# A Conformer-like layer on eight cores: four fill banks, adds on GpSimd, an early load of x, conv weights made on the chip, and conv results taken over DRAM

## The chip, the cores and the metric

The kernel runs on all 8 cores of one Trainium2 chip (dies: cores 0 to 3 and 4 to 7). Each core computes half of one of four sequences, 2048 frames plus what it needs of the past. The metric is the device time of the slowest core, in microseconds (us). Some executions of a program on all 8 cores are disturbed: a pair of cores or a whole die gets a lower TensorE clock and takes longer. I therefore quote two things: the ratio of fast runs, and the median span of the *undisturbed cores*, by which I mean, in runs of state fast, the cores whose granted clock is within 0.012 of the highest of that run. (A run's state is slow when one die is over 1% longer than the other at a lower clock, or when the run is over 1.5% above the fastest of its kernel. So a fast run can still hold a disturbed pair.)

## The reference, cut

```python
def reference(x, ...):                                   # x: (4, 4096, 1024) float32
    x = x + 0.5 * swiglu(rmsnorm(x, ffn1_norm), ffn1_gate, ffn1_up, ffn1_down)   # hidden 2816
    z = rmsnorm(x, mix_norm) @ w_in                      # q, k, v (512 each) and [a | b] for the conv
    attn_out = chunk_band_attention(q, k, v, rel_bias)   # 8 heads of 64, 576-key band, softmax
    conv_out = conformer_conv(u, ...)                    # GLU -> causal conv, width 31 -> LayerNorm -> silu
    x = x + concatenate([attn_out, conv_out]) @ w_out
    x = x + 0.5 * swiglu(rmsnorm(x, ffn2_norm), ffn2_gate, ffn2_up, ffn2_down)
    return rmsnorm(x, final_norm)
```

## The kernel before

The program holds a small scheduler. Each part of the layer (a norm, the GLU, an attention, ...) is a Python generator that yields a function "when could I go on?"; the scheduler estimates engine times with a simple model and lets the ready generator of the highest priority emit its next instructions. The result is a fixed order on each engine, with semaphores where data is handed over. If the model is wrong about a landing, an engine stands behind the wrong instruction. A core takes its frames in two groups (group 0 and group 1), each of them through the first FFN (FFN1), GLU, conv, attention, output projection and second FFN (FFN2). Weights pass through a ring in SBUF, loaded by a queue that GpSimd issues.

The norm: ScalarE squares, VectorE adds, TensorE sums over partitions, ScalarE makes the root, VectorE normalises eight tiles in one go.

```python
        def square(st, g, kc, s):
            ...
            act(sqt, xsl(g, kc, s), AF.Square, n, (xk,), (("sq", i),))
            if k < 7:
                dve(lambda h: h.tensor_tensor(out=ss, in0=ss, in1=sqt, op=ALU.add), n, ...)
        def norm_fin(st, g, s, idx):
            yield lambda: P.est("pe", (("ssb", r),), (("ps", 6 + nxt("st", 2, False)),))
            b = 6 + nxt("st", 2)                          # two fill banks: 6 and 7
            mm(b, 0, onesS, ssb_t[:, r, 0:n], n, True, True, ...)
            ...
            yield lambda: P.est("dve", (("rstd", rr),)) - 0.3
            for kc in range(8):                           # eight in one go
                dve(... scalar_tensor_tensor(hT or y <- x * gain * rstd) ...)
```

The LayerNorm of the conv's result, with its Silus and the way back to channel order:

```python
        def conv_ln(g):
            ...
            yield lambda: P.est("act", (("acc", 7),)) - 0.2
            for grp in range(16):                         # one burst, before the attention
                act(co[:, grp, 0:U], acc[:, grp, 0:U], AF.Silu, ...)
            for pc in range(2):                           # 32 small transfers in SBUF, as 32 before the conv
                for p4 in range(4):
                    for j in range(4):
                        P.dma("sp", ... c2 <- co ...)
            for s in g.main:
                for c in range(4):
                    dve(... tensor_copy: cvt <- c2 ...)   # to frame order, for the output projection
```

And the attention, in units: scores of two heads (64-row matmuls in pairs), exp on ScalarE, values on TensorE; at the end of a pair of heads the row sums go through Ln and Exp on ScalarE to a reciprocal, and VectorE multiplies. It could start only when the LayerNorm had read its two accumulator banks (flag ln45).

Names in the lines of the profile: `psA` are the four PSUM banks of gate, up and attention scores, `ps` the four others, among them the *fill banks* that all other matmuls share; `hT` is the normalised x, `xres` the x that is carried along, `sq`, `ssum` and `ssb` are squares and their sums, `rstd` is the reciprocal root made of them, `ring` holds weights, and `dreg` is a scratch region that GLU, conv and attention use in turn. PEld is the weight load of TensorE.

The softmax here doesn't subtract the row's maximum and nothing guards it: scores larger than these inputs give would overflow.

## Time and profile before

| before | |
|---|---|
| median of all 16 runs in the end | 1619.0 us (1614.9 to 1803.7) |
| a fast run | 1615 to 1621 us |
| profiled run | fast, cores 1594.8 to 1612.8 us |
| TensorE busy, idle | 1446.6 us (90%), 166 us |
| ScalarE table loads | 37 of 1283 ns |

The profile is read from the top down: the busy line names the bound (TensorE), the slices say where it has holes, the windows by stage give each hole a size, and the waits and the chain give each a cause. The lines are in the prediction below.

### The profile page before, as it was taken

How to read it: one execution, taken by the hardware profiler on the slowest of the kernel's cores; microseconds unless marked ns; L12 is line 12 of the kernel's file. 1: busy time of each engine (PE TensorE's matmuls, PEld its weight loads, DVE VectorE, ACT ScalarE, POOL GpSimd, SP SyncE). 2: the span in 40 equal slices, each digit the busy share in tenths (PEclk: the TensorE clock that was granted, in tenths of full speed). 3: DMA queues.
4: the chain of work that ended last, by engine and by line, in shares of the span. 5: the costliest groups of instructions: out<-in, count | busy, mean ns of one | idle time of the engine just before them, and what ended most of it. 6: DMA issues, size and time to landing. Idle time of an engine off the chain costs nothing.

```text
span 1612.8 us, 22367 instructions; the slowest of 8 cores (1594.8 to 1612.8 us)
## 1 busy us (share of the span) xinstructions
PE 1446.6 (90%) x8206; PEld 772.9 (48%) x8206; DVE 597.0 (37%) x1005; ACT 464.8 (29%) x791; POOL 52.1 (3%) x102
## 2 busy tenths in 40 slices
PE   4599999987688999986899999999888899999995
PEld 1255555444444466642455555445334455555542
DVE  3522222464323522256322222674533542222145
ACT  2311011231446410144310011333556631101122
POOL 0000000000000000000000000000000000000000
PEclk9799999999798999998899999999999999999997
DMA  8334215147630266518144232055610033343303
GB/s 176 93 73 85 53 27 92 27 105 124 122 69 1 53 111 111 99 37 231 23 76 86 53 65 54 11 114 105 128 37 1 1 65 60 55 78 58 66 1 130
DMA packets 26905, 119.21 MB, mean 74 GB/s; under 512 B 8112, under 2 KB 12208, under 8 KB 16816
## 3 DMA queue, kind: packets, MB, share of 16 engines
q0 software_dynamic: 14112, 93.33, 32.7%
q1 hardware_dynamic: 12688, 24.47, 4.6%
q8 instruction: 68, 1.11, 0.3%
q14 instruction: 37, 0.30, 0.1%
HBM read 198.49 MB, written 8.39 MB: 128 GB/s over the span
## 4 chain that ended last, share of the span: by engine, by line
PE 73%; DVE 9%; ACT 7%; issue 5%; DMA 5%; SPq 2%; DVEq 0%; ACTq 0%; POOL 0%; POOLq 0%
PE psA L352 45%; PE ps L352 28%; ACT dreg L356 3%; DVE hT L506 2%; DMA xres<-xin 2%; DMA ring<-wgu 2%; SPq L728 1%; ACT L356 1%; DVE ssum L466 1%; ACT sq L356 1%; DVE xres L647 1%; DVE dreg L506 1%; DMA dreg<-dreg 1%; ACT rstd L356 1%; DVE dreg L997 1%
## 5 line engine op out<-in xcount | busy, mean ns | idle before, releaser
L352 PE MATMUL psA<-hT,ring 128*128 128x384 bf16 (+2 forms) x4192 | 770.7, 345 | 25.8 <-DVE hT L506 20.3
L352 PEld LDWEIGHTS psA<-hT,ring 128*128 128x128 bf16 x4192 | 413.0, 99 | 378.5 <-issue 59.8
L356 ACT ACTIVATE dreg<-psA 128x384 f32<-128x384 f32 (+4 forms) x346 | 216.8, 631 | 773.0 <-PE psA L352 761.1
L352 PE MATMUL ps<-at,ring 128*128 128x384 bf16 (+1 forms) x1936 | 357.5, 346 | 20.1 <-DVE xres L647 20.1
L617 DVE TENSOR_TENSOR at<-psA,dreg 128x384 bf16<-128x384 f32 (+1 forms) x242 | 143.6, 594 | 517.2 <-PE psA L352 502.6
L352 PEld LDWEIGHTS ps<-at,ring 128*128 128x128 bf16 x1936 | 191.2, 99 | 184.0 <-issue 36.5
L647 DVE SCALAR_TENSOR_TENSOR xres<-ps,xres 128x384 f32<-128x384 f32 (+1 forms) x176 | 104.8, 596 | 153.6 <-PE ps L352 153.6
L356 ACT ACTIVATE sq<-xres 128x384 bf16<-128x384 f32 (+1 forms) x154 | 84.5, 552 | 180.2 <-DVE xres L647 134.8
L466 DVE TENSOR_TENSOR ssum<-ssum,sq 128x384 f32<-128x384 f32 (+1 forms) x132 | 78.5, 595 | 92.4 <-ACT sq L356 87.2
L352 PE MATMUL ps<-dreg,ring 128*128 128x384 bf16 (+3 forms) x608 | 98.3, 313 | 1.1 <-DVE xres L1054 0.6
L506 DVE SCALAR_TENSOR_TENSOR hT<-xres,cs_sb,rstd 128x384 bf16<-128x384 f32 (+1 forms) x136 | 78.8, 653 | 11.9 <-ACT rstd L356 11.9
L352 PE MATMUL ps<-hT,ring 128*128 128x384 bf16 (+1 forms) x352 | 69.8, 356 | 12.0 <-ACT at L356 6.0
L352 PEld LDWEIGHTS ps<-dreg,ring 128*128 128x128 bf16 x608 | 58.1, 101 | 30.7 <-issue 3.5
L356 ACT ACT_TABLE_LOAD x37 | 47.5, 1283 | 45.8 <-PE psA L352 25.5
L352 PE MATMUL ps<-dreg,at 128*128 128x384 bf16 (+3 forms) x216 | 45.4, 307 | 16.4 <-DVE dreg L997 10.3
L352 PEld LDWEIGHTS ps<-hT,ring 128*128 128x128 bf16 x352 | 35.1, 101 | 42.6 <-issue 18.7
L352 PE MATMUL ps<-ssb,cb_sb 128*128 128x384 bf16 (+1 forms) x22 | 8.3, 379 | 49.2 <-DVE ssb L471 49.2
L420 POOL DMA_DIRECT2D ring<-wgu x44 | 23.4, 533 | 822.5 <-PE ps L352 503.5
L356 ACT ACTIVATE dreg<-dreg 128x192 bf16<-128x192 f32 (+5 forms) x88 | 35.4, 440 | 48.7 <-DVE dreg L844 44.8
L720 DVE TENSOR_TENSOR dreg<-psA,dreg 128x384 bf16<-128x384 f32 (+2 forms) x20 | 39.5, 1995 | 16.4 <-PE psA L352 8.7
L997 DVE TENSOR_TENSOR dreg<-ps,dreg 64x384 bf16<-64x384 f32 (+1 forms) x40 | 23.3, 581 | 59.1 <-ACT dreg L356 56.5
L352 PE MATMUL ps<-ring,hT 128*128 128x512 bf16 x160 | 37.5, 391 | 4.1 <-DVE vh L665 3.0
(56 smaller groups left out, 446.4 us busy)
## 6 DMA issues: line engine op xcount, KB each, us to landing
ring<-wgu POOLq DMA_DIRECT2D x44, 1024.0 KB, 9.7
ring<-wdA POOLq DMA_DIRECT2D x16, 768.0 KB, 7.7
ring<-wdB POOLq DMA_DIRECT2D x16, 640.0 KB, 7.0
ring<-win POOLq DMA_DIRECT2D x10, 1024.0 KB, 9.2
ring<-wcv POOLq DMA_DIRECT2D x8, 1152.0 KB, 11.2
xres<-xin SPq DMA_DIRECT2D x4, 1536.0 KB, 18.6
yout<-dreg SPq DMA_DIRECT2D x3, 1536.0 KB, 6.3
ring<-wout POOLq DMA_DIRECT2D x4, 1024.0 KB, 16.7
```

The costliest lines, as they stand in the source:

```text
L352: P.op("pe", lambda h: h.matmul(o, lhsT=lhsT, rhs=rhs, start=start, stop=stop, skip_group_check=True), max(n / 2370.0, 0.06) if dur is Non ...
L356: P.op("act", lambda h: h.activation(out=out, in_=in_, func=func, **kw), 0.19 + n / 1400.0, reads, writes)
L420: P.dma("pool", lambda h, dst=dst, src=p.src: h.dma_start(out=dst, in_=src), "w%d" % (p.id % 8), 512 * p.n, reads=(), writes=(("w", p.id), ...
L466: dve(lambda h: h.tensor_tensor(out=ss, in0=ss, in1=sqt, op=ALU.add), n, (("ssum", r), ("sq", i)), (("ssum", r),))
L506: dve(lambda h, dst=dst, xin=xin, gcol=gcol: h.scalar_tensor_tensor(out=dst, in0=xin, scalar=gcol, in1=rt, op0=ALU.mult, op1=ALU.mult), n, ...
L617: dve(lambda h, at=at, ub=ub, tt=tt: h.tensor_tensor(out=at, in0=ub, in1=tt, op=ALU.mult), n, (("ps", bU), ("tmpF", ti)), (("AT", gi, fl, ...
L647: dve(lambda h, xo=xo, bk=bk: h.scalar_tensor_tensor(out=xo, in0=bk, scalar=0.5, in1=xo, op0=ALU.mult, op1=ALU.add), n, (("ps", b), xk), ( ...
L720: dve(lambda h, gd=gd, a4=a4, t4=t4: h.tensor_tensor(out=gd, in0=a4, in1=t4, op=ALU.mult), n, (("ps", bA), ("rs", ti)), (("g", c),))
L728: P.dma("sp", lambda h, src=src, dst=dst: h.dma_start(out=dst, in_=src), "gp%d" % pc, 64 * 2 * W, reads=(("g", 2 * pc), ("g", 2 * pc + 1)) ...
L997: dve(lambda h, o_=o_, i0=i0, i1=i1: h.tensor_tensor(out=o_, in0=i0, in1=i1, op=ALU.mult), n, (("ps", 4 + e), ("rs", ri)), (("q", gi, j, s),))
```

## The change

Its intent is to fill TensorE's holes. Its parts: (1) four fill banks instead of two, and normalising in steps of two tiles; (2) the adds of the sums of squares move from VectorE to GpSimd (Pool), save in the first norms; (3) the x of group 1 is loaded early into free scratch and normalised from there; (4) the 64 small transfers per group between GLU, conv and output become 24 larger ones over DRAM; (5) the conv's weights are no longer loaded but multiplied out of 576 columns, half on Pool, half on VectorE; (6) the conv's sums go to Pool instead of through 64 statistics matmuls; (7) the order is freer: the attention no longer waits for ln45, the first block's V and Q rank right behind the conv, and the Silus are given out in pairs; (8) dummy matmuls keep the clock up where the model foresees a gap. Besides, x and some of the weights arrive in smaller pieces. Cut to its core:

```diff
+        mode = {"fill": (4, 5, 6, 7), "lru": [4, 5, 6, 7]}          # (1); 6, 7 during attention
-            b = 6 + nxt("st", 2)
+            b = fb_take()
...                                                                  # norm_fin
-            yield lambda: P.est("dve", (("rstd", rr),)) - 0.3
             for kc in range(8):
+                if kc % 2 == 0:
+                    yield lambda: max(P.est("dve", (("rstd", rr),)) - 0.3, P.t["dve"] - 1.0)
...                                                                  # square (2)
+            add = dve if norm0 and g.gi == 0 else pool
...                                                                  # (3)
+        def prefetch_x(g):
+            yield lambda: 0.0 if ("wout", g.gi - 1) in F else INF
+            for s in g.ids[1:]:
+                P.dma("sp", ... xps <- xin ...)
+                S.add(0, norm_load(g, s))
...                                                                  # conv_ln (4), (7)
-            yield lambda: P.est("act", (("acc", 7),)) - 0.2
             for grp in range(16):
+                if grp % 2 == 0:
+                    yield lambda: max(P.est("act", (("acc", grp + 1),)) - 0.2, P.t["act"] - 1.0)
                 act(co[:, grp, 0:U], acc[:, grp, 0:U], AF.Silu, ...)
-            ... 32 transfers c2 <- co
+            ... 8 transfers to DRAM, 4 back (likewise for GLU to conv)
...                                                                  # attention (7)
-                    if ("Q", gi, s) not in F or ("v", gi, s) not in F or ("ln45", gi) not in F:
+                    if ("Q", gi, s) not in F or ("v", gi, s) not in F:
...                                                                  # issue_weights (5)
+                    (pool, dve)[p.src % 2](... ring <- cmp * identity, 2304 wide ...)
...                                                                  # mm (8)
+            keep_warm(gap, b)
```

## The prediction

> **What bounds the kernel now.** I read the table of cores first, to know the state: this execution is a fast one (both dies within 0.4%), so its 1612.8 us is what a fast run takes (the two fast runs: 1614.94 and 1615.3). Then the busy line, the slices, the costliest groups, the windows by stage, the waits of TensorE, and the chain and timeline around the big holes.
>
> ```profile
> PE 1446.6 (90%) x8206; PEld 772.9 (48%) x8206; DVE 597.0 (37%) x1005; ACT 464.8 (29%) x791; POOL 52.1 (3%) x102
> PE   4599999987688999986899999999888899999995
> PEclk9799999999798999998899999999999999999997
> ```
> PE is the bound, but the holes sit in a few places: the start, slices 8 to 13, 17 to 20, 26 to 31 and the end, and the clock dips in the same slices.
>
> ```profile
> 0.00:70.00 70.00, 30.65 (x106) 11.42 (x106) 28.29 (x55) 23.25 (x39) 2.46 (x8) 0.85 0.69 155
> 296.00:348.00 52.00, 44.71 (x239) 23.47 (x238) 32.50 (x56) 16.78 (x28) 1.05 (x2) 0.97 0.39 92
> 348.00:437.00 89.00, 64.74 (x413) 39.70 (x412) 40.33 (x55) 27.02 (x63) 4.22 (x8) 0.90 0.60 102
> 437.00:560.00 123.00, 108.03 (x687) 55.01 (x684) 47.22 (x87) 67.82 (x105) 2.11 (x4) 0.90 0.25 49
> 697.00:800.00 103.00, 80.73 (x381) 38.89 (x382) 55.00 (x100) 41.74 (x68) 2.11 (x4) 0.85 0.38 98
> 1003.00:1060.00 57.00, 52.41 (x270) 26.21 (x269) 36.23 (x59) 20.11 (x31) 1.59 (x3) 0.97 0.27 52
> 1060.00:1155.00 95.00, 88.34 (x501) 47.64 (x498) 56.41 (x62) 38.05 (x75) 4.22 (x8) 1.00 0.61 109
> 1155.00:1300.00 145.00, 120.87 (x819) 58.93 (x820) 57.70 (x99) 88.22 (x123) 1.06 (x2) 0.93 0.11 24
> 1547.00:1613.00 66.00, 45.75 (x225) 23.26 (x223) 39.14 (x68) 17.13 (x30) 0.00 (x0) 0.84 0.20 80
> ```
> Columns: stretch, its length, busy PE, weight load, DVE, ACT, POOL, then granted clock, DMA share, GB/s. The stages are, in order: start; end of the first FFN; GLU and conv of group 0; its attention; the change from group 0 to group 1; then for group 1 the end of FFN1, GLU and conv, attention; and the tail. Length less busy gives the idle time: 39.4, 7.3, 24.3, 15.0, 22.3, 4.6, 6.7, 24.1, 20.3 us, together 164 of the 166 us in the whole run. The FFN stretches between them are full, at clock 1.00.
>
> ```profile
> PE ps L352 <- DVE ssb L471: 49.2, 11, 18.0
> PE ps L352 <- ACT dreg L356: 28.7, 26, 12.5
> PE psA L352 <- DVE hT L506: 20.3, 32, 4.4
> PE ps L352 <- DVE xres L647: 20.1, 12, 5.3
> PE ps L352 <- DVE dreg L997: 15.7, 20, 2.3
> ```
> Columns: who waited for whom, total us, times, longest. The first line is PE waiting for the sum of squares of a norm; in truth it waits for x, as the chain says at the change of groups (20.24 us of loading x, then squares):
>
> ```profile
> 733.50 20.24 DMA xres<-xin
> ```
> The longest wait on ACT is the conv of group 0, for which the 32 small transfers from GLU order to phase order take from 367.6 to over 400 us:
>
> ```profile
> 408.68 0.57 PE L352 MATMUL ps<-dreg,cb_sb 128*128 128x192 bf16 x2 [12.47 <-ACT dreg L356]
> ```
> And the fourth line is a blocked bank: DVE writes eight normalised tiles in one go, in order, and PE stands until the accumulator is added to x:
>
> ```profile
> 1570.17 5.38 DVE L506 SCALAR_TENSOR_TENSOR dreg<-xres,cs_sb,rstd 128x512 f32<-128x512 f32 x8
> 1576.17 9.04 PE L352 MATMUL ps<-at,ring 128*128 128x384 bf16 x40 [5.26 <-DVE xres L647]
> ```
>
> **What the Trainium skill says.** (1) "TensorE: Matmul & The Clock Gate", Part 1: a warm matmul starts every N/2.4 + 2.5 ns, and after an idle window of about 3.4 us the clock halves until some 3.4 us of work have passed. The trace agrees: in one dense down-projection the chain holds 288 matmuls in 51.92 us, 180.3 ns each, and the formula for the mean width of 426.7 gives 180.3. After the first hole the weight loads of 512-wide matmuls start 0.43 us apart, then 0.21. (2) "GPSIMD Engine Reference", 3.1: an elementwise add of two fp32 inputs takes 4497 ns for 2048 elements there against 2293 on VectorE. No run here shows it (Pool does no adds yet); my estimate from it is 0.85 to 1.0 us at 384 wide, against 595 ns measured on DVE. (3) "SBUF — State Buffer", "Who interferes with whom": a DVE instruction with two SBUF inputs and a Pool instruction that reads SBUF exclude each other. The 8-tile normalisation is such a DVE instruction; silu products and residual adds read PSUM and are not. (4) "DMA: Bandwidth & Descriptors", anatomy of a DMA: about 2 us fixed per transfer. The trace's shortest GLU transfer lands in 1.9 us.
>
> **The floor.** Over all forms, count times (N/2.4 + 2.5 ns) sums to 1370 us; the 64-row score matmuls (35 us of it) run in pairs, so about 1355. 1613 - 1355 = 258 us are lost: 166 idle, the rest slow clock and small matmuls. Slow clock I estimate per stage as busy x (1 - clock): 4.6, 1.3, 6.5, 10.8, 12.1, 1.6, 0, 8.5, 7.3, sum 53 us. So 217 us lie within the change's reach.
>
> **The change part by part.** Each line: idle + slow clock now, what I leave after.
> - Start (39.4 + 4.6, leave 37 + 3): x arrives in quarters, blocks 1 and 2 in halves, and the Ln of a norm no longer queues behind the squares of the next block. But some 15 MB of x, weights and tables must still come in before blocks 1 and 2 can run, and the ring still holds four FFN pieces. Gain 4.
> - End of FFN1, both groups (11.9 + 2.9, leave 5 + 0): normalisation now in steps of two tiles (2 x 0.65 us) instead of eight, and four accumulator banks instead of two, so the 5.3 us block goes. Gain 10.
> - GLU and conv (31.0 + 6.5, leave 11 + 2): 64 small transfers per group (32 in, 32 back) become 24 larger ones over DRAM: per group 8 writes and 4 reads for GLU, 8 and 4 for conv. About 0.6 us issue each, two latencies, perhaps 10 us in all, under K's matmuls (24 x 3 remaining at some 0.19 us, 14 us). The conv weights (8 x 1152 KB at 11.2 us) are no longer loaded but multiplied out, half on Pool (2304 elements, estimate 5 us), half on DVE (2304/0.96, 2.4 us), 4 each per group, ahead of use. The 64 statistics matmuls (formula 7.0 us) and 32 ACT copies go; 15 pairs of Pool adds per group replace them. Gain 24 + 7.
> - Attention (39.1 + 19.3, leave 24 + 8): it no longer waits for the conv's LayerNorm banks, and conv, V and Q fill it. Its own chain of scores, exp (1.03 us each), values and reciprocal (waits of 2.0 to 2.3 us on L997) stays. Gain 26.
> - Change of groups (22.3 + 12.1, leave 4 + 2): x of blocks 1 and 2 of group 1 is loaded into the free scratch during FFN2 and normalised before the old x is gone. The 20.24 us load leaves the path. Gain 28.
> - Tail (20.3 + 7.3, leave 11 + 2): the bank stalls of 5.26 and 3.66 us go; from the last product to the output (1602 to 1613) it stays. Gain 15.
> - 154 sum-of-squares adds (91.6 us) leave DVE except 24 in the first norms; off the path, save the last of each norm: + 0.4 us x about 12 = 5.
> - Dummy matmuls fill gaps that the scheduler's own model foresees, to hold the clock. Where the model is wrong they delay real work: + 4.
>
> Sum: 4 + 10 + 31 + 26 + 28 + 15 = 114, less 9: 105 to 108. 1613 - 108 = 1505.
>
> **The rivals.** *Pool becomes the hidden bound.* It would carry some 130 adds x 1 us, 60 conv adds x 0.6, 8 x 5 us of weights: about 220 us, 14% of the span, but bunched: at the change of groups 40 adds x 1 us against 26 us of down-projection, in order with the weight transfers it issues. For: in-order queue, shared port. Against: three FFN pieces of block 0 (20 us) can run meanwhile. It would give back 20 to 30 us: 1525 to 1535. *The dummies and the scheduler's model miss.* The order on PE is fixed beforehand; if real landings differ, PE stands behind the wrong item or 90 dummies. For: at the start the model counts on a constant written earlier than the trace's 4.9 us. Against: there PE waits for data anyway. 1530 to 1560. *All holes close.* Fillers suffice and the clock stays full: floor 1348 + start 40 + tail 11 + small-matmul loss 30 + 30 = 1460. *Nothing moves:* the DRAM detour and ACT's exp replace each wait by another; against it, the 20 us load and the 5.3 us blocks go by data dependence, not by luck.
>
> **Range and chances.** 1505 us for a fast run; 1463 (near the best case) to 1558 (second rival) should hold it 8 times in 10. For "within 2%" three quarters of the gain must be lost, though the parts are independent: 4%. Slower by over 2%: 2%. Faster by over 2%: 94%. In the slow state, which two of the four runs before had, all is longer; I predict the fast one.
>
> **What would show it.** Right: no x load in the chain at the change of groups; waits on xres under 1 us; no 12 us hole before conv; PE waits on the sum of squares only at the start; Pool near 15% busy; busy PE higher than 90% of the span, with a new group of 256-wide matmuls (dummies); clock over 0.97 in the attention stages. Wrong: Pool adds over 1.3 us, or PE waits on Pool of several us per norm; gu weights landing late because their issue queues behind adds; attention stages as long as before (123 and 145 us with the same matmuls); the start longer than 70 us.

## The result and the profile after

| | before | after |
|---|---|---|
| median, all runs | 1619.0 us (16 runs) | 1558.6 us (11 runs, 1533.5 to 1773.5) |
| runs with no disturbed core | 1614.9 to 1621 | 1533.47, 1533.58, 1536.68, 1536.69 |
| undisturbed cores, median | 1609 | 1530 |
| ratio of the fast runs | | 0.9515 [0.9475, 0.9556] |

The result was correct and the change is faster. Ratios in this document are the mean time of one kernel's fast runs over that of the other's fast runs of the same rounds, so not quite the ratio of the quoted medians. The run that was profiled is disturbed on cores 6 and 7 only (1551.9 and 1557.1 us at clock 0.967 and 0.965; the others 1527.5 to 1534.0), so from here I compare core 0 with core 0: 1603.3 us before, 1529.4 after.

The page of the kernel after, its busy line and the slices of the clock:

```profile
PE 1470.7 (94%) x8558; PEld 810.6 (52%) x8558; DVE 554.9 (36%) x886; ACT 458.2 (29%) x758; POOL 276.8 (18%) x313
...
PEclk9999999999999999998888999999989999999998
```

TensorE fills 94% of a shorter span (91% without the dummies), and Pool went from 3% to 18%. The dips of the clock around the conv and the attention of group 0 are gone. Those in slices 19 to 22 lie on the disturbed core whose page this is, core 0 has none there; the one in slice 30, in the attention of group 1, core 0 has too. Groups of instructions that the change made or touched, after and (last two lines) before; columns: line, engine, operation, tiles, shapes, count, busy us, mean ns of one, idle before and its cause:

```profile
L569 POOL TENSOR_TENSOR ssum<-ssum,sq 128x384 f32<-128x384 f32 (+1 forms) x114 | 121.0, 1061 | 192.1 <-ACT sq L418 183.9
L606 DVE SCALAR_TENSOR_TENSOR hT<-xres,cs_sb,rstd 128x384 bf16<-128x384 f32 (+1 forms) x120 | 87.5, 781 | 9.4 <-ACT rstd L418 9.4
L405 PE MATMUL ps<-cb_sb 128*128 128x256 bf16 x412 | 50.4, 282 | 4.9 <-DVE cb_sb L1237 4.9
```

```profile
L506 DVE SCALAR_TENSOR_TENSOR hT<-xres,cs_sb,rstd 128x384 bf16<-128x384 f32 (+1 forms) x136 | 78.8, 653 | 11.9 <-ACT rstd L356 11.9
```

A Pool add takes 1.06 us (predicted 0.85 to 1.0 at a width of 384; at that width it is 1.01 on core 0, the mean has wider ones in it). The normalising product on VectorE went from 653 to 781 ns. These means mix widths; for the same form on core 0 it is 612 to 678 ns at 384 and 746 to 975 at 512. That Pool's reading is the cause is shown by the run addsdve below: with the adds off Pool the two are 611 and 744 again. L405 are the dummies, 50 us of TensorE that is no work. The waits of TensorE on core 0 after (who waited for whom, us, times, longest):

```profile
PE ps L414 <- ACT dreg L418: 19.0, 15, 6.4
PE ps L414 <- POOL ssb L574: 17.8, 9, 2.7
PE ps L414 <- DVE dreg L1133: 11.7, 19, 4.3
PE ps L414 <- DVE dreg L970: 8.7, 3, 5.9
```

The wait for x behind VectorE's sums (47.9 us on this core before) and the one for a blocked bank (DVE xres, 19.6 us before) have left the top of the list. But for the first this holds in part only: 27.2 of the 47.9 us were in the first 70 us, where x arrives, and there the dummies now cover the wait. Without them (run nowarm below) 29.3 us stand in the same place. What leads now is ScalarE in the attention, then Pool.

**Where the time went, stage by stage.** Because V and the end of the conv now run inside the attention, the lengths of stages can't be compared. So I take the loss of each stage: its length less the ideal time of the real matmuls in it, which is the count of each shape times (N/2.4 + 2.5 ns), half for the 64-row pairs, and nothing for dummies. Stage borders are from core 0's timeline, to about 1 us; FFN1 ends with its last down-projection. The prediction took its numbers from core 7, the slowest one, so its column is compared to about that. The spans fell by 79 us in the median of the undisturbed cores, by 74 on core 0, which was a short one before.

| stage | loss before | after | gain | predicted |
|---|---|---|---|---|
| start, up to the first down-projection | 42.2 | 43.4 | -1 | 4 |
| FFN1 from its first down-projection, both groups | 17.6 | 5.8 | 12 | 10 |
| norm, GLU, K and conv, both groups | 46.1 | 24.4 | 22, and 7 of matmuls that went | 31 |
| attention and output projection, both groups | 80.5 | 75.3 | 5 | 26 |
| FFN2 of group 0 and start of FFN1 of group 1 | 34.4 | 16.5 | 18 | 28 |
| FFN2 of group 1 and output | 26.2 | 14.3 | 12 | 15 |
| sum | 247.0 | 179.7 | 74 | 114 less 9 |

74 us is the difference of the two spans. The attention is the large miss. Windows of core 0 over the attentions of groups 0 and 1, first before, then after (length; busy us of PE, weight load, DVE, ACT, Pool; clock; DMA share; GB/s):

```profile
445.00:518.00 73.00, 58.16 (x427) 29.17 (x427) 22.96 (x44) 45.06 (x63) 0.53 (x1) 0.90 0.13 27
1155.00:1275.00 120.00, 103.33 (x722) 50.14 (x720) 47.76 (x82) 77.57 (x105) 0.53 (x1) 0.91 0.07 14
```

```profile
412.00:485.00 73.00, 60.62 (x476) 31.83 (x475) 22.36 (x40) 59.16 (x82) 4.99 (x8) 0.98 0.44 80
1086.00:1215.00 129.00, 112.29 (x808) 56.91 (x805) 57.06 (x80) 95.90 (x129) 17.39 (x17) 0.96 0.23 46
```

The clock did what was predicted: 0.90 and 0.91 became 0.98 and 0.96, and busy time beyond the ideal fell from 15.6 + 23.0 to 9.9 + 17.1 us, 11.6 in all (predicted 11.3). But the idle time, with the dummies of 5.5 and 4.2 us counted as idle, went from 14.8 + 16.7 = 31.5 up to 17.9 + 20.9 = 38.8. The prediction's step from 39.1 to 24 is for longer windows, with output projection in them; with the whole output projections (445 to 598 and 1155 to 1395 us before, 412 to 570 and 1086 to 1333 after) core 0 went from 35.2 up to 46.8, where the prediction had it fall by 15. And ScalarE has 14 and 18 us more to do in the attentions.

What ScalarE does there, from its timeline in group 1 after (start, us, engine, line, operation, tiles, shapes, count), with the matmul of TensorE that waited:

```profile
1101.98 2.29 ACT L418 ACTIVATE dreg<-dreg,cs_sb 128x320 bf16<-128x320 f32 x4
1104.29 1.28 ACT L418 ACT_TABLE_LOAD   x1
1105.58 1.21 ACT L418 ACTIVATE dreg<-ps 64x512 f32<-64x512 f32 x2
...
1108.44 1.31 PE L414 MATMUL ps<-dreg,vh 128*128 128x512 bf16 x2 [6.39 <-ACT dreg L418]
```

and of before, where the same Silus ran ahead of the attention:

```profile
1134.53 1.28 ACT L356 ACT_TABLE_LOAD   x1
1135.82 8.82 ACT L356 ACTIVATE dreg<-dreg,cs_sb 128x320 bf16<-128x320 f32 x16
```

The Silus come in four bursts (2, 4, 6 and 4 of them) between the exps of the attention. Before each burst a table is loaded and after it another: 8 loads of 1.28 us in each attention, where before there were 2 per group, one ahead of the burst and one at the attention's first exp. The reciprocal (two Ln of 64 rows) stands behind such a burst, and behind the reciprocal both VectorE's product and ScalarE's next exp. The values of the next heads need the bank that the product frees and the result of that exp; TensorE stood 6.39 us and started 0.02 us after the exp's end at 1108.42. The diff has it in one line, the yield in front of every second Silu, and I had read over it.

### The profile page after: what moved, and what is told of

It reads as the page before. It is cut to its first block, busy times and chain, and to the rows that moved or that the text cites. A ratio compares the mean times of both kernels' runs of the same rounds, so it can differ in the third digit from the quotient of the medians.

```text
span 1557.1 us, 23493 instructions; the slowest of 8 cores (1527.5 to 1557.1 us)
## 1 busy us (share of the span) xinstructions
PE 1470.7 (94%) x8558; PEld 810.6 (52%) x8558; DVE 554.9 (36%) x886; ACT 458.2 (29%) x758; POOL 276.8 (18%) x313
## 4 chain that ended last, share of the span: by engine, by line
PE 81%; DVE 5%; issue 5%; ACT 5%; POOL 2%; DMA 1%; DVEq 0%; SPq 0%; POOLq 0%; ACTq 0%
PE psA L414 51%; PE ps L414 28%; ACT dreg L418 3%; DVE hT L606 2%; PE ps L405 2%; POOL ssum L569 1%; ACT L418 1%; DVE xres L748 1%; DVE dreg L606 1%; DVE dreg L1133 1%; ACT rstd L418 1%; DMA dreg<-gscr 0%; ACT sq L418 0%; POOL ssb L574 0%; DVE ssum L569 0%
## 5 line engine op out<-in xcount | busy, mean ns | idle before, releaser
L418 ACT ACTIVATE dreg<-psA 128x512 f32<-128x512 f32 (+4 forms) x346 | 216.8, 632 | 791.3 <-PE psA L414 775.0
L569 POOL TENSOR_TENSOR ssum<-ssum,sq 128x384 f32<-128x384 f32 (+1 forms) x114 | 121.0, 1061 | 192.1 <-ACT sq L418 183.9
L418 ACT ACTIVATE sq<-xres 128x384 bf16<-128x384 f32 (+1 forms) x140 | 76.9, 555 | 125.7 <-DVE xres L748 77.5
L606 DVE SCALAR_TENSOR_TENSOR hT<-xres,cs_sb,rstd 128x384 bf16<-128x384 f32 (+1 forms) x120 | 87.5, 781 | 9.4 <-ACT rstd L418 9.4
L414 PE MATMUL ps<-hT,ring 128*128 128x384 bf16 (+1 forms) x352 | 65.9, 344 | 0.0
L418 ACT ACT_TABLE_LOAD x41 | 52.6, 1283 | 43.0 <-PE psA L414 18.5
L405 PE MATMUL ps<-cb_sb 128*128 128x256 bf16 x412 | 50.4, 282 | 4.9 <-DVE cb_sb L1237 4.9
L405 PEld LDWEIGHTS ps<-cb_sb 128*128 128x128 bf16 x412 | 41.3, 101 | 12.0 <-issue 5.0
L503 POOL DMA_DIRECT2D ring<-wdA x16 | 8.4, 529 | 213.5 <-PE psA L414 213.5
L495 POOL TENSOR_TENSOR ring<-cmp_sb,cb_sb 128x2304 bf16<-128x2304 bf16 x8 | 33.5, 4191 | 47.9 <-PE psA L414 42.0
## 6 DMA issues: line engine op xcount, KB each, us to landing
ring<-wout POOLq DMA_DIRECT2D x4, 1024.0 KB, 13.5
```

What stands on the lines that cost most here:

```text
L405: P.op("pe", lambda h: h.matmul(o, lhsT=onesS, rhs=cb[:, B_ONES:B_ONES + 256], start=True, stop=True, skip_group_check=True), 0.11, ("cb1" ...
L414: P.op("pe", lambda h: h.matmul(o, lhsT=lhsT, rhs=rhs, start=start, stop=stop, skip_group_check=True), max(n / 2370.0, 0.06) if dur is Non ...
L418: P.op("act", lambda h: h.activation(out=out, in_=in_, func=func, **kw), 0.19 + n / 1400.0, reads, writes)
L495: lambda h, o_=o_, i0=i0, i1=i1: h.tensor_tensor(out=o_, in0=i0, in1=i1, op=ALU.mult), p.n,
L503: P.dma("pool", lambda h, dst=dst, src=src: h.dma_start(out=dst, in_=src), "w0" if p.id == 0 else "w%d" % (1 + p.id % 16), 512 * w, reads= ...
L569: add(lambda h: h.tensor_tensor(out=ss, in0=ss, in1=sqt, op=ALU.add), n, (("ssum", r), ("sq", i)), (("ssum", r),))
```

## The experiments

Twelve kernels ran, all derived from the kernel after. Median span of the undisturbed cores, to be compared with 1530 us of the kernel after (its own range over cores is 1525 to 1535), and the ratio of fast runs to before, to be compared with 0.9515:

| run | undisturbed cores | ratio to before |
|---|---|---|
| silu16 | 1545 | 0.9572 [0.951, 0.9634] |
| gate | 1540 | 0.9546 [0.9484, 0.9608] |
| cvdma | 1533 | 0.9658 [0.9609, 0.9707], disturbed pair in each run |
| nowarm | 1536 | 0.9512 [0.9451, 0.9573] |
| expln (wrong) | 1512 | 0.9372 [0.9351, 0.9392] |
| halfexp (wrong) | 1528 | none, one fast run |
| nopref | 1549 | 0.9611 [0.9594, 0.9628] |
| smalldma | 1526 | 0.9527 [0.9447, 0.9607] |
| silulate | 1518 | 0.9418 [0.9405, 0.9432] |
| addsdve | 1565 | 0.9695 [0.9677, 0.9713] |
| ht8 | 1555 | none given |
| ht8two (wrong) | 1593 | 0.9979 [0.996, 0.9998] |

The disturbed pairs widen the ratios of the kernel after, cvdma and smalldma, and nowarm has only two fast runs, so for those I go by the cores.

**silu16: the Silus in one burst.** My theory was that their alternation with the exps keeps TensorE idle.

```diff
-                if grp % 2 == 0:
-                    yield lambda: max(P.est("act", (("acc", grp + 1),)) - 0.2, P.t["act"] - 1.0)
+                if grp == 0:
+                    yield lambda: max(P.est("act", (("acc", 15),)) - 0.2, P.t["act"] - 1.0)
```

> The changed kernel, but the 16 Silu of the conv's LayerNorm in one burst instead of in bursts of 2, 4, 6 and 4 between the exps of attention. Theory A (table switches: each burst is bracketed by two table loads of 1.28 us and the exps behind them come late, so attention got longer): table loads fall from 41 to about 29, PE's waits on ACT from 19 us to under 12, and the time falls by 6 to 14 us from the 1535 us of the changed kernel's fast runs. Theory B (attention is held by its own chain of scores, exp, values and reciprocal, and by a lack of other matmuls): the table loads fall all the same, the time stays within 3 us.

Ten loads went (41 to 31) and TensorE's wait on ScalarE fell from 19 to 11.8 us, but the kernel became 15 us slower. VectorE's timeline in group 0 (core 1) shows what came in their place:

```profile
438.85 1.14 DVE L1133 TENSOR_TENSOR dreg<-ps,dreg 64x384 bf16<-64x384 f32 x2 [1.36 <-ACT dreg L418]
457.56 3.57 DVE L1045 COPY dreg<-dreg 128x384 bf16<-128x384 bf16 x8 [17.56 <-DMA dreg<-cscr]
```

The copies of the conv's result wait for the way over DRAM, and VectorE stands 17.6 us at them with the attention's product behind. The scheduler had put them there because its model has the data back about 12 us after the last Silu (its own times, from running its code); in truth the copies could start 34 us after it. In that time four weight pieces of 1 MB were under way on the same DMA engines; that they are the cause is likely, but no run took them away. So this run moved two things and settled nothing about the loads.

**gate: the same, and the attention waits for the Silus.**

```diff
+            F.add(("ln", gi))                      # after the 16 Silus
-                    if ("Q", gi, s) not in F or ("v", gi, s) not in F:
+                    if ("Q", gi, s) not in F or ("v", gi, s) not in F or ("ln", gi) not in F:
```

> The same single burst of Silu, and attention starts only once that burst is issued, much as in the kernel before. Theory A: the burst no longer sits ahead of any exp; as fast as the burst alone or up to 5 us better, if V and Q fill PE meanwhile. Theory B: PE has too little else to do while it waits for the LayerNorm: 3 to 10 us slower than the burst alone.

1540 us, 5 less than silu16, as theory A allowed, and still 10 more than the kernel after. VectorE stood 13.6 us at the copies again, TensorE waited 21.6 us for the products behind them, and the first score of group 0 came about 5 us later. With the copies in the way, the old order does not make the new kernel better.

**cvdma: the conv's weights loaded again, 8 transfers per group.**

```diff
-            addp((gi, "cv", i), i, 2304)
+            addp((gi, "cv", i), wcv_d[i], 2304)
```

> The changed kernel, but the conv weights are loaded as before (8 pieces of 2304 columns per group) instead of multiplied out on Pool and VectorE. Theory C (the products cost VectorE 4 us each where I had put 2.4, they shut out and are shut out by Pool's reads, and they hold up the conv's bank evacuation): PE's wait on the conv evacuation, 8.7 us in three waits, falls under 2 us, and the time falls by 5 to 9 us. Rival: the 9.4 MB more to load delays the GLU reorder, V or the output projection: the time stays within 3 us or rises by up to 10.

1533 us on undisturbed cores: no gain and no loss of weight. What the multiplication costs is seen in the kernel after, core 0: of the two products of VectorE shown the first overlaps Pool's and takes 9.60 us, the other 3.04 (the median of all eight is 2.63), and the conv's evacuation waits behind it.

```profile
1048.81 9.60 DVE L495 TENSOR_TENSOR ring<-cmp_sb,cb_sb 128x2304 bf16<-128x2304 bf16 x1
1051.95 4.04 POOL L495 TENSOR_TENSOR ring<-cmp_sb,cb_sb 128x2304 bf16<-128x2304 bf16 x1
1059.02 3.28 PE L414 MATMUL ps<-dreg,ring 128*128 128x320 bf16 x12 [5.89 <-DVE dreg L970]
1059.26 3.04 DVE L495 TENSOR_TENSOR ring<-cmp_sb,cb_sb 128x2304 bf16<-128x2304 bf16 x1
```

With loaded weights this wait goes, and one for the GLU's way over DRAM (4.1 us) and other small ones take its place.

**nowarm: no dummy matmuls.**

```diff
-            if gap < 0.8 or gap > 100 or "cb1" not in P.lastw:
+            if True or gap < 0.8 or gap > 100 or "cb1" not in P.lastw:
```

> The changed kernel without the dummy matmuls (412 of them, 50 us of PE). Theory D (they only fill holes, and what they hold is the clock at the start of the work after): mean granted clock falls from 0.986 to about 0.97, the time rises by 3 to 10 us, nearly all in the first 70 us. Rival E (they stand in the way: at the start they end after the first weights are there): the first FFN matmul comes at 23 us instead of 25.5 and the time falls by up to 3 us, or stays.

1536 us at a clock of 0.973 instead of 0.985. The 50 us of dummies are worth about 6 us net. What they delay is in that: at the start the first FFN matmul comes at 25.49 us with them and at 24.85 without. I had charged 4 us for delays; the run can't tell these from the gain.

**expln: the 32 Silus computed as Exp.** This keeps every shape and, checked line by line, the order on every engine; only the table loads go. Its output is wrong, which doesn't matter for the time.

```diff
-                act(co[:, grp, 0:U], acc[:, grp, 0:U], AF.Silu, U, ...
+                act(co[:, grp, 0:U], acc[:, grp, 0:U], AF.Exp, U, ...
```

> Wrong result on purpose: the 32 Silus of the conv's LayerNorm are computed as Exp instead, the function that the attention around them uses, so that no table has to be loaded between them; same shapes, same order on every engine. Theory A (the alternation of Silu and Exp on ScalarE, 10 table loads of 1.28 us in each attention, is what keeps TensorE idle there): the waits of TensorE on ScalarE in the attention fall from 19.0 us to under 10, the two attentions (73 and 129 us on an undisturbed core) get 12 to 20 us shorter together, undisturbed cores end at 1510 to 1518. Theory B (each unit's own chain of scores, exp and values waits, and there is no filler left): table loads fall by 20 or so, the time by at most 5 us: 1524 to 1530. The simulator's order is the same, so an effect of order on VectorE, as with the one burst, cannot hide it.

1512 us, 18 less than the kernel after. Core 0 has 25 loads instead of 41, so 16 x 1.28 = 20.5 us of ScalarE's time went, and its attentions take 66 and 116 us instead of 73 and 129:

```profile
413.00:479.00 66.00, 60.25 (x470) 32.05 (x470) 21.99 (x39) 48.10 (x74) 4.96 (x8) 0.97 0.49 89
1077.00:1193.00 116.00, 107.02 (x792) 55.62 (x801) 56.69 (x80) 84.18 (x121) 16.89 (x17) 1.00 0.24 51
```

TensorE's wait on ScalarE falls from 19.0 to 4.2 us. The idle time with dummies is 66 - 60.25 + 5.5 and 116 - 107.02 + 4.2, together 24.4 instead of 38.8. (Some 20 matmul records are missing in these two windows, some 4 us, so it is rather less.) With the output projections it is 32.8 instead of 46.8, and these stages take 385 us instead of 405: 20 of the 21 us that the prediction missed there. Theory A holds, on runs in which the order can't be the cause: the scheduler's model charges both functions the same, so it gives the same order.

**halfexp: exp of one head of each pair only**, the other half filled with ones. Its output is wrong, which doesn't matter for the time. It asks whether the unit's own chain is the limit.

```diff
-                    act(Pb[:, pi, :, 0:w], src, AF.Exp, 2 * w, ...
+                    act(Pb[:, pi, 0:1, 0:w], src[:, 0:1, :], AF.Exp, 2 * w, ...
+                    dve(lambda h: h.memset(Pb, 1.0), ...)          # once per group
```

> Wrong result on purpose: the exp of each attention unit is taken of one of its two heads only (half the elements, about 0.6 us instead of 1.03), the other half of the tile is filled with ones once per group; same order on every engine, same table loads. Theory B (the unit's own chain of scores, exp and values): 84 exps, each 0.4 us shorter, most of it seen by TensorE: 20 to 30 us less, undisturbed cores at 1500 to 1510. Theory A (table switches): the loads stay, so only the exps that follow one gain; 5 to 10 us less. A third way: VectorE (evacuations, normalising) or the ratio of small matmuls is the limit, then under 5 us.

1528 us, 2 less, though an exp of two 512-wide halves takes 0.60 us instead of 1.02. My note that the order stays was wrong: the memset shifted the order on TensorE somewhat, and group 1 got 10 loads instead of 8. So the run doesn't measure the exp cleanly. It does say that 30 us less ScalarE work in the two attentions (155.05 to 125.37 us busy), with the loads left in, bought next to nothing, while expln's 23 us less bought 20. This points away from how much ScalarE works, and to the burst between two loads that stands ahead of a reciprocal; as the order moved, it is a hint and no proof.

**silulate: one burst, and the model told the truth about the landing.** The theory after silu16 and expln together: the burst pays if VectorE gets the copies later.

```diff
+                if grp == 0:                                    # as in silu16
-                      issue=0.6, total=4, late=4.0)             # way back, c2 <- DRAM
+                      issue=0.6, total=4, late=20.0)
```

> Candidate for a version that beats both. The Silus of the conv's LayerNorm in one burst (10 table loads fewer than the changed kernel, as in the first run of this kind), and the scheduler's model told that the way back of the conv's result over DRAM takes 16 us longer than it assumed (with the real landing 34 us after the last Silu), so that VectorE gets the copies that wait for it behind the normalising products of the attention, not in front of them. If the wait of VectorE at those copies was what ate the first run's gain, as its trace showed (17.6 us in group 0): the attentions come to some 66 and 118 us, undisturbed cores to 1510 to 1520, ratio to the changed kernel 0.985 to 0.993. If the burst itself is what costs (7 and 9 us of ScalarE in which no exp runs): 1528 to 1540 as before.

Correct, 1518 us, and 0.9418 of before: it beats both kernels, and its interval lies below that of the kernel after. VectorE's timeline of core 0 at the same place as above:

```profile
461.67 1.14 DVE L1133 TENSOR_TENSOR dreg<-ps,dreg 64x384 bf16<-64x384 f32 x2 [6.17 <-ACT dreg L418]
462.84 3.61 DVE L1045 COPY dreg<-dreg 128x384 bf16<-128x384 bf16 x8
```

The copies come after the products and wait for nothing. The attentions take 68 and 122 us:

```profile
414.00:482.00 68.00, 60.98 (x483) 33.16 (x481) 21.75 (x39) 51.21 (x77) 5.17 (x8) 0.97 0.50 86
1080.00:1202.00 122.00, 109.74 (x802) 56.23 (x801) 56.50 (x80) 87.23 (x122) 17.15 (x17) 0.97 0.23 48
```

Loads in them are 2 and 2 instead of 8 and 8. The loss of attention and output projection is 65.0 us instead of 75.3, so the gain there is 15 of the 26 predicted.

**nopref: x of group 1 loaded when the old x is gone**, as before the change.

```diff
-            if g.gi == 1 and s > 0:
+            if False:
-        S.add(9, prefetch_x(G[1]))
```

> The early load of x for group 1 is undone, all else stays. Predicted worth of the part: 28 us; the stage accounting of the changed kernel says 18 (loss of the change of groups 34.4 before, 16.5 now). If the early load is the cause of those 18 us: 15 to 25 us slower, undisturbed cores at 1545 to 1555, ratio to the changed kernel 1.010 to 1.016, and the load of x back in the chain of waits at the change of groups, with a hole of 10 to 20 us at TensorE. If the scheduler's freedom (more fill banks, three FFN pieces of block 0 first) covers it anyway: under 5 us.

1549 us, 19 more. The loss at the change of groups is some 38 us on core 0 instead of 16.5, and the load is back in the chain of waits (first line; start, us, what) and in TensorE's timeline (second):

```profile
689.69 19.80 DMA xres<-xin
```

```profile
718.39 0.48 PE L414 MATMUL ps<-ssb,cb_sb 128*128 128x384 bf16 x1 [11.08 <-POOL ssb L573]
```

So the early load is the cause of the gain of 18 there. Why 18 and not 28? In the kernel after, TensorE's two causes of waiting in FFN2 of group 0 are ScalarE's rstd (5.1 us once) and Pool's sums (4.9 us in two), 10 us together. Pool does the adds of the new x and of the last residuals back to back, one every 1.12 us, and ScalarE's squares are paced by it, with a norm's Ln in line behind them:

```profile
672.29 0.92 POOL L569 TENSOR_TENSOR ssum<-ssum,sq 128x384 f32<-128x384 f32 x1 [0.20 <-POOL ssum L569]
673.41 0.91 POOL L569 TENSOR_TENSOR ssum<-ssum,sq 128x384 f32<-128x384 f32 x1 [0.20 <-POOL ssum L569]
```

```profile
683.45 6.59 PE L414 MATMUL ps<-at,ring 128*128 128x384 bf16 x30 [5.15 <-ACT rstd L418]
```

(The first two lines are from Pool's timeline, the last from TensorE's.) That is my first rival, bunched adds, at a third to a half of the size I gave it. It is read from the waits; no run took these adds away alone.

**addsdve: the adds back on VectorE.** The question was whether Pool's waits are worth undoing.

```diff
-            add = dve if norm0 and g.gi == 0 else pool
+            add = dve
```

> The adds of the sums of squares back on VectorE (114 of 1.06 us on Pool become 114 of some 0.6 us on VectorE), all else stays. TensorE now waits 17.8 us for Pool's last adds (9 waits of 2 us). If moving the adds to Pool cost what I charged for it (5 us) and the waits are Pool's slowness: those waits halve, 3 to 9 us faster, undisturbed cores at 1521 to 1527. The rival, that VectorE needs the relief: its own queue delays the products and evacuations, waits on DVE hT and at grow, 5 to 15 us slower.

1565 us, 35 more, on all cores alike in all four runs where they were undisturbed. Both of my sides missed: VectorE's sums now hold TensorE for 23.0 us where Pool's held it 17.8. The loss grows by 8 and 7 us in the two stages of norm, GLU, K and conv, by 7 at the change of groups, where TensorE stands 10.6 us at an addition to x, and by 13 at the very end, where 14 normalising products in a row precede a wait for an output transfer. Part of that is order, which the model chose anew with the other durations; the run doesn't separate order from load. It does say that the rest of the change needs VectorE relieved: I had put this part down as a cost of 5 us and nothing else.

**smalldma: the 32 + 32 small transfers per group again.**

```diff
-                src = d_[:, :, s4, :]
-                dst = gp[32 * s4:32 * s4 + 32, :, u0:u0 + W]
+                for j in range(4):
+                    src = gT[32 * j:32 * j + 32, 2 * pc:2 * pc + 2, s4, 0:W]
...                                                       # likewise c2 <- co
```

> The detour over DRAM is undone: GLU order to phase order and back goes by 32 + 32 small transfers per group directly between partitions, as before; all else stays. If the many small transfers were the cause of the conv's hole: back come 8 to 20 us, of it most in group 0's GLU and conv (79 us now) as a wait of TensorE of some 10 us in front of the conv, ratio to the changed kernel 1.005 to 1.013. The rival: K, V and Q as fillers hide either way: within 3 us. A second rival: two hops over DRAM take longer than one, and the change loses by it: 2 to 5 us faster.

1526 us, 4 less, as the second rival had it, but at the edge of what the cores tell apart. The way over DRAM is not what closed the hole of 12 us in front of the conv: with the small transfers back, the hole doesn't come back. The traces say how it arose: on core 7 before, VectorE's evacuation of the conv waited 13.5 us (until 407.60) for these transfers, because the accumulators lie over the GLU's tile that the transfers read. In smalldma the last of the 32 is issued by 377.5 us and the conv's first matmul comes at 378.8, so that no evacuation waits for them; before, core 0 started the conv at 381.7 and issued until 384.5. What brought this about, the freed banks, the order of V and Q, or something else, no run separates.

**ht8two and ht8: eight tiles in one go, with and without only two fill banks.**

```diff
-                if kc % 2 == 0:
+                if kc == 0:                                       # both
-        mode = {"fill": (4, 5, 6, 7), "lru": [4, 5, 6, 7]}
+        mode = {"fill": (6, 7), "lru": [4, 5, 6, 7]}              # ht8two only, and after the attention
```

> Two parts undone together, the normalisation in steps of two tiles and the four fill banks (back to eight in one go and two banks). Predicted worth of them: 10 us at the ends of the first FFN and 15 in the tail; the stage accounting says 11.8 and 11.9. If they are the cause: 15 to 25 us slower, undisturbed cores at 1545 to 1555, with waits on DVE xres of 3 to 5 us back at TensorE, and the loss in the FFN1 and FFN2 stages up by as much, nowhere else. If the early Ln and the finer weight pieces did it: under 6 us.

> One half of the pair undone alone: the normalisation in one go of eight tiles, the four fill banks stay. The pair together was 64 us slower on core 0 and gave a wrong result. If the eight in one go are the main cost (VectorE closed for 8 x 0.7 us while a bank waits): 25 to 45 us slower, undisturbed cores at 1555 to 1575. If four banks absorb it, as the scheduler intends, and the two banks were the main cost: under 15 us slower, 1530 to 1545. A correct result would put the error of the pair down to the two banks or their combination.

The pair took 1593 us, 63 more, and its result was wrong (relative error 0.16). ht8 alone is correct at 1555 us, 25 more, so the error belongs to the two banks or the combination, and I have not found it. I rest little on its time: TensorE's waits for a blocked bank are back as expected (18.4 us in 13 waits on core 0, against 19.6 before), yet the loss is up in nearly all stages (11 us in FFN1, 14 in GLU and conv, 18 in attention and output projection, 10 at the change, 9 in the tail), not only where I looked for it. The finer steps alone are worth 25 us in this kernel, as much as the two stages gained in which I had booked both parts. But they are not worth it there: with four banks and eight tiles in one go TensorE waits only 4.2 us for a blocked bank, and by my estimate (the loss as in the table, corrected for some 90 missing matmul records) some 16 of core 0's 23 us fall on GLU and conv and on the change of groups, some 5 on the two booked stages. Parts of this change lean on each other, and undoing one in the new kernel is not the mirror image of adding it to the old.

## Why the prediction was right or wrong

The class (faster by over 2%) was right, and fast runs lie in the range. The point was 1505 us; a run without a disturbed core takes 1533 to 1537, so some 30 us are missing. (114 less 9 is 105; the point took 108. The adds that stay on VectorE are 21, not 24. Neither matters.) Of its own signs of being wrong one came true: the attentions take 73 and 129 us where they took 73 and 120. By its own steps:

- **Start, gain 4:** measured -1. As the prediction said itself, it is bound by transfers; the pieces of x didn't change that.
- **End of FFN1, gain 10, and tail, gain 15:** measured 12 and 12. Waits on xres left the list, as predicted; of its two causes the four banks did most of that, since ht8 with eight tiles in one go has 4.2 us of them and before had 19.6. What the finer steps bring lies mostly in other stages.
- **GLU and conv, gain 24 + 7:** measured 22 + 7. The number was right by luck as far as it rests on the larger transfers: smalldma shows that they weren't it. A conv weight product on VectorE took 2.63 us in the median, near the 2.4 of the sum, but 9.60 where it met Pool.
- **Attention, gain 26:** measured 5. This is the step that failed. It is "Attention (39.1 + 19.3, leave 24 + 8)", and in it the idle term: the clock's 11.3 came as 11.6, but idle, attention with output projection on core 0, went from 35.2 up to 46.8 instead of down by 15. The prediction let the attention start before the conv's LayerNorm was done, and didn't count what comes with it: 16 Silus inside the attention of each group, and with the yield in front of every second one 8 table loads. expln takes away the loads alone and gets 18 us, with that idle time at 32.8; silulate gets 12 with a correct result.
- **Change of groups, gain 28:** measured 18, with the mechanism (no x load in the chain) shown by nopref at 19. The missing 10 are, by the waits, Pool's bunched adds and the Ln behind them, which I had named as a rival and not put in the sum; that is read, not shown by a run.
- **Costs, 5 for the later last adds and 4 for dummies:** TensorE waits 17.8 us for Pool's sums in nine places, more than 5, but without Pool it is 35 us worse, and the dummies bring 6 net, their delays included.

The misses (-21 attention, -10 change, -5 start, -3 tail, +2 and -2) turn the 114 of the stages into 75; 74 were measured. The 9 of costs lie inside the measured stages.

## What to carry to other kernels

When a change lets two stages overlap, list what each engine other than the bound gets in the overlap, and in which order: on ScalarE, functions of two table sets that alternate cost a load at each turn, and here the chain behind them weighed more than their sum of time. A scheduler's model must know the real latency of a transfer that runs beside large loads, or an in-order engine is made to stand at a copy with the urgent work behind it. Check a theory with an experiment that can't move the order (another function, same shape): the run that changed loads and order together pointed the wrong way.

## What the Trainium skill lacked or had wrong

- "ScalarE: Activation LUTs", "What ACT_TABLE_LOAD costs", gives about 1283 ns for the load and about 1380 ns of drain, some 2.66 us for a switch. The load is 1.28 us here too, but no drain shows: the Silus end at 1104.27, the load runs from 1104.29, and the next activation starts at 1105.58. Taking 16 loads away shortened core 0 by 22 us and ScalarE's busy time by 21.9, 20.5 of it the loads, so 1.3 us a switch is the figure to plan with here. The advice under "Rules for kernel authors", to group calls by table set, is what this change went against.
- "GPSIMD Engine Reference", 3.1: an estimate of 0.85 to 1.0 us for a 384-wide add came from its figures. Undisturbed an add takes 0.91 us, the mean with wider ones is 1.06. What the section lacks is the pace of dependent adds: 0.20 us between one and the next, so one every 1.12 us.
- "SBUF — State Buffer", "Who interferes with whom": that a VectorE instruction with two SBUF inputs contends with Pool's reads agrees with the trace. What the section lacks is how long a row of Pool instructions can hold VectorE: a product took 9.60 us that began with five of them back to back (1048.81 to 1055.99 on core 0), and 2.56 where Pool stood still.
- "DMA: Bandwidth & Descriptors" lacks the time to landing of a small transfer beside large loads. Here transfers of 96 and 160 KB to DRAM, issued by SyncE, landed after 1.9 to 21.3 us on core 1 (silu16: up to 26.2), with weight pieces of 1 MB under way.
